# A transformer block on one core: one product for the bias rows of four heads, and two weight blocks split by another engine

## The chip, the cores and the metric

The kernel runs on one core of a Trainium2 chip. The time is that of one execution on the device, in microseconds (us). Three executions took 1603.33, 1603.94 and 1609.25 us; the median is 1603.94.

The core has a matrix engine (TensorE, PE in the profile; its weight loads are PEld), a vector engine (VectorE, DVE), a scalar engine (ScalarE, ACT), a general engine (GpSimd, POOL) and an engine that only issues DMAs (SyncE, SP). Each takes its own instructions in order; between engines semaphores order the work. TensorE's clock is granted at one of two levels, 1.2 and 2.4 GHz; the profile's "PEclk" is the granted share of the higher one.

## The reference, cut to what matters

One decoder layer for 512 tokens of width 1024, all in fp32:

```
a = rmsnorm(x);  dq, dk, dv, rq, rk, rv, rg = split(a @ w_in)
A = differential attention of 4 heads (dq, dk, dv), causal,
    logits + rel_bias[t5_bucket(distance), head]
B = retention of 4 heads (rq, rk, rv), gated by silu(rg)
h = x + concat(A, B) @ w_out
m = rmsnorm(h);  h += peer(m):  scores of m @ Wq against sub-keys, two top-16 lists,
    top-16 of their sums, softmax, sum over experts of gelu(m . u_e) * g_e * v_e
h += sigmoid(rmsnorm(h) @ Wg + bg) * (p @ Wp);  out = rmsnorm(h)
```

The attention's bias depends on the head and on the distance of the two tokens alone. So each head has one row of 640 numbers, a value for each distance, and the 128x512 bias tile of a head is that row, shifted by one place from line to line.

## The kernel before, in words

Every large product is made of three: both operands are split into a high part (a rounded copy, made by ScalarE) and a low part (the rest, a subtraction), and high x high, high x low and low x high are added in PSUM. A weight block (512 KB) is loaded by SP, split, and used by 24 products of 128x512; while one block is multiplied, the next is split (cut_high on ScalarE, cut_low on VectorE) and one further is loaded. The order of each engine's instructions is written out by hand.

After the value projection and the first query projection (project_tile, L214; its products are made at L85), rr holds each token's scale; ScalarE copies it to rT and scales the values (keep_values, L280 to L283). Then come **the bias rows** (L336 to L342). The table relx holds the bias of each bucket and head on 33 partitions, and bucket0 and bucket512 hold for each of 640 distances which bucket it is in (a one for that bucket). relw repeats one head's column of relx 128 times, so that the product of relw[:, h] with the bucket table is the bias row of head h, the same on 128 partitions. For each head there are two products, of 512 and of 128 columns (plain fp32, which TensorE makes in two passes, so two instructions each), into PSUM tiles from a ring of two; ScalarE copies both into bias_s, and POOL's queue writes bias_s to bias_d[h] in DRAM. Later the function table (L375 to L378) loads bias_d[h] back through POOL's queue, with a step of 639 between lines, which makes the shifted 128x512 tile toep; VectorE adds it to the scores (L388).

Then three more projections follow (L344 to L347), each with its scaled copy out of PSUM (keep_dqk, L330 to L333), its split on ScalarE and VectorE, and for queries also two casts on POOL (stack_q, L302). With the second round of steps the attention loop begins: it interleaves the steps of further projections with the scores of one head and 128 queries (scores_of, L380; products at L322).

The query projection of the expert part (**Wq**) has 16 blocks, used from L945 on. Blocks 0 and 1 are loaded and prepared ahead of it, in the output projection, with VectorE. In the loop over blocks, prepare (L735) is called for a block that is two ahead: ScalarE makes the high part (L745), and the low part is made in one of two ways. With `low` = VectorE it is one subtraction (L761). With `low` = GpSimd ScalarE writes the negated block to wl (L758) and POOL issues a DMA that adds the raw block to it (L759):

```
if low is nc.gpsimd:
    nc.scalar.activation(wl, w, AF.Copy, scale=-1.0)
    nc.gpsimd.dma_start(wl.bitcast(F32), w, accum_op=OP.add)
else:
    low.tensor_tensor(wl, w, wh.bitcast(F32), op=OP.subtract)
```

Each turn of the loop then multiplies a block (products, L765), copies its result to qt (ScalarE, L980), multiplies the block before with its sub-keys (score, L948 to L954) and ranks the one before that (rank, top-16 lists on VectorE).

Of the kernel before, what the change touches and what calls it, by code (L numbers as in the profile page):

```python
# [23 lines left out]
F32 = mybir.dt.float32  # L24
# [5 lines left out]
AF = mybir.ActivationFunctionType  # L30
# [5 lines left out]
P = 128  # L36
# [18 lines left out]
def block_kernel(ctx: ExitStack, tc, t):  # L55
    nc = tc.nc

    def pool(name, bufs=1, **kw):
        return tc.tile_pool(name=name, bufs=bufs, reuse_waits="tile", **kw)
# [36 lines left out]
    def operand():  # L96
        return [[ops.tile([P, S], F32R, name=f"x{z}{k}", tag=f"x{z}{k}") for z in "hl"] for k in range(KC)]

    def scaled_split(h, lo, src, gain):

        nc.scalar.activation(h, src, AF.Copy, scale=gain)
        nc.vector.scalar_tensor_tensor(lo, src, gain, h.bitcast(F32), op0=OP.mult, op1=OP.subtract)
# [39 lines left out]
    bias_d = dram.tile([4, P, 640], F32, name="bias_d")  # L142
    blk = [slice(b * P, (b + 1) * P) for b in range(4)]
    halves = [slice(0, S), slice(S, D)]
    with pool("wa", 2, side="right") as wa, pool("sm", 2, side="right") as sm, \
# [67 lines left out]
        with pool("proj", side="right") as pj, pool("att", 2, side="right") as at:  # L213
            def project_tile():  # L214
                ps = mm.tile([P, S], F32, name="ps", tag="mm")
                project(ps, take(), xa, slice(0, S))
                ahead()
                return ps


            relx = pj.tile([33, 4], F32, name="relx")
            nc.gpsimd.memset(relx, -1.0e30)
            nc.gpsimd.dma_start(relx[:32], t["rel_bias"])
            bucket = [(at.tile([33, c1 - c0], F32, name=f"bucket{c0}", tag=tag, **kw), c0, c1)
                      for c0, c1, tag, kw in ((0, 512, "rp", {}), (512, 640, "rx", {"bufs": 3}))]
# [3 lines left out]
            for i, n in enumerate(("lam_q1", "lam_k1", "lam_q2", "lam_k2")):  # L229
                x = t[n]  # L230
# [8 lines left out]
            def fetch_x(i):  # L239
                x = at.tile([P, 2, S], F32, name="pr", tag="pr", bufs=3)  # L240
                if i > 0:
                    nc.sync.dma_start(x, t["xT"][:, 2 * i:2 * i + 2])
                else:
                    raw_w[0] = wa.tile([P, 2, S], F32, name="wraw", tag="wraw")
                    for z in range(2):
                        nc.sync.dma_start(x[:, z], t["xT"][:, z])
                        nc.sync.dma_start(raw_w[0][:, z], blocks[0][0][:, z])
                return x

            steps[:] = 1, 1, 1  # L250
            x = fetch_x(0)
            cut_w[0] = [wa.tile([P, 2, S], F32R, name="w" + z, tag="w" + z, bufs=3) for z in "hl"]
            for i in range(4):
# [8 lines left out]
                x = nx  # L262
# [20 lines left out]
                    nc.scalar.activation(val[which, b], ps[b], AF.Copy, scale=ra[:, b:b + 1])  # L283

            first_q = project_tile()
            relw = at.tile([33, 4, P], F32, name="relw", tag="rp")
            nc.vector.tensor_copy(relw, relx[:, :, None].to_broadcast([33, 4, P]))
            rr = psM.tile([P, S], F32, name="rr", tag="misc")
            token_rows(at.tile([P, 4, P], F32, name="dg", tag="rx", bufs=3), rr, ra)
            rT = pj.tile([P, S], F32, name="rT")  # L290
# [42 lines left out]
                dqk[a, m, z] = yield from (stack_q, stack_k)[z](m, x)  # L333


            for h in range(4):  # L336
                bias_s = at.tile([P, 640], F32, name="bias_s", tag="pr", bufs=3)
                for x, c0, c1 in bucket:
                    pb = psM.tile([P, 512], F32, name="pb", tag="misc")
                    nc.tensor.matmul(pb[:, :c1 - c0], relw[:, h], x, start=True, stop=True)  # L340
                    nc.scalar.activation(bias_s[:, c0:c1], pb[:, :c1 - c0], AF.Copy)
                nc.gpsimd.dma_start(bias_d[h], bias_s)  # L342

            for m, z in ((0, 1), (1, 0), (1, 1)):  # L344
                ps = project_tile()
# [243 lines left out]
            for n in range(17):  # L589
                if n < 16:  # L590
                    h, qb = n // 4, n % 4
# [59 lines left out]
            for n in range(16):  # L651
                h, b = n // 4, n % 4
# [82 lines left out]
        def prepare(u, low):  # L735
            kind, i = u
            w = raw.pop(u)
            if kind == "g":
                for d in range(2):
                    c = slice(d * S, (d + 1) * S)  # L740
                    scaled_split(fin["gh"][i][d], fin["gl"][:, i, c], w[:, c], gains[:, G_PLE, i:i + 1])
                return
            wh = wt.tile([P, D], F32R, name="wh", tag="wh")
            wl = wt.tile([P, D], F32R, name="wl", tag="wl")
            nc.scalar.activation(wh, w, AF.Copy)  # L745
            parts[u] = wh, wl
            if kind == "v":
                gv, av = inputs.pop(u)
                if gv is not None:
                    av3 = av.rearrange("p (z t) -> p z t", t=RUN)  # L750
                    nc.vector.tensor_tensor(av3, gv, av3, op=OP.mult)
                ah = vp[0].tile([P, ND], F32R, name="ah", tag="ah", bufs=2)
                al = vp[0].tile([P, ND], F32R, name="al", tag="al", bufs=2)
                nc.scalar.activation(ah, av, AF.Copy)  # L754
                parts[u] += ah, al
# [6 lines that stand above are left out]
            if kind == "v":  # L762
                nc.vector.tensor_tensor(al, av, ah.bitcast(F32), op=OP.subtract)  # L763
# [157 lines left out]
    with pool("pk") as pk, pool("psG", 2, space=PSUM) as psG, pool("psT", space=PSUM) as psT:  # L921
# [3 lines left out]
        def top16(lists):  # L925
            for v, ix, src, tmp in lists:
                nc.vector.max(v[:, 0:8], src)
            for v, ix, src, tmp in lists:
                nc.vector.match_replace(tmp, v[:, 0:8], src, NEG)
            for v, ix, src, tmp in lists:  # L930
                nc.vector.max(v[:, 8:16], tmp)
            for v, ix, src, tmp in lists:
                nc.vector.max_index(ix[:, 0:8], v[:, 0:8], src)
            for v, ix, src, tmp in lists:
                nc.vector.max_index(ix[:, 8:16], v[:, 8:16], tmp)
# [7 lines left out]
        with pool("qs", 2) as qs:  # L943
            units = [("q", c) for c in range(16)] + [("u", n) for n in range(RAW - 1)]
            loaded, prepared = 2, 2  # L945
            sks, qt, scores = {}, {}, {}

            def score(c):  # L948
                sc = psT.tile([P, 4, P], F32, name="sc", tag="sc")
                for b in range(4):  # L950
                    nc.tensor.matmul(sc[:, b], qt[c][:, b * P:(b + 1) * P], sks[c], start=b == 0, stop=b == 3,  # L951
                                     skip_group_check=True)
                scores[c] = qs.tile([P, 4, P], F32, name="scs", tag="scs", bufs=3)
                nc.scalar.activation(scores[c], sc, AF.Copy)  # L954

            def rank(c):
                ic = qs.tile([P, 4, TOPK], U32, name="ic", tag="ic")
                for b in (0, 2):
                    top16([(vals[:, z, c], ic[:, z], scores[c][:, z],
                            pk.tile([P, P], F32, name="tmp", tag="tmp", bufs=2)) for z in (b, b + 1)])  # L960
                nc.vector.tensor_copy(idx[:, :, c], ic)

            for c in range(16):
                while loaded < min(len(units), c + RAW):
                    load(units[loaded])
                    loaded += 1
                while len(sks) < min(16, c + RAW):
                    k = len(sks)
                    sks[k] = qs.tile([P, P], F32, name="sk", tag="sk", bufs=RAW + 1)
                    nc.sync.dma_start(sks[k], t["sk_t"][k])  # L970
                while prepared < min(len(units), c + 3):
                    prepare(units[prepared], nc.gpsimd if units[prepared][0] == "q" else nc.vector)
                    prepared += 1
                if c == 0:
                    nc.vector.tensor_copy(io2, iof[:, :, None].to_broadcast([P, P, 2]))
                    nc.vector.tensor_copy(pairs.rearrange("p z a k -> p (z a) k"),
                                          prf[:, :3 * TOPK, None].to_broadcast([P, 3 * TOPK, TOPK]))
                products(("q", c))
                qt[c] = qs.tile([P, S], F32, name="q", tag="q")
                nc.scalar.activation(qt[c], made.pop(("q", c)), AF.Copy)  # L980
                if c:
                    score(c - 1)
                if c > 1:
                    rank(c - 2)
            score(15)
            rank(14)
            rank(15)
# [195 lines left out]
        while busy or later or after or n % QUAD:  # L1183
# [23 lines left out]
            while (writes and n >= made_at[writes[0][2]] + 2 and clock["dma"] + LOAD <= clock["pe"] + SLACK):  # L1207
                f, q, g = writes.pop(0)
# [103 lines left out]
    with pool("acc", space=PSUM) as pa:  # L1312
# [43 lines left out]
        loaded, prepared = RAW - 1, 2  # L1356
# [13 lines left out]
        for n, u in enumerate(seq):  # L1370
            while loaded < min(total, n + RAW):
# [4 lines left out]
                if kind == "g" and "gh" not in fin:  # L1376
                    x = operand()
# [10 lines left out]
            if writes and n % W_EVERY == 0:  # L1388
                f, q, g = writes.pop(0)
# [13 lines left out]
            if 0 <= n - end_at < len(ends):  # L1403
                name, b = ends[n - end_at]
# [100 lines left out]
```

## Time and profile before

| | |
|---|---|
| median of three executions | 1603.94 us |
| profiled execution, its own time | 1605.48 us |
| its span, first to last instruction | 1603.7 us |
| mean granted TensorE clock | 0.985 |
| TensorE busy | 1542.4 us, 96% |
| VectorE busy | 1222.3 us, 76% |
| ScalarE busy | 678.9 us, 42% |
| GpSimd busy | 376.2 us, 23% |
| chain that ended last | PE 64%, DMA 13%, issue 11%, DVE 7%, POOL 2%, ACT 2% |

The profile is one execution. A row of the timeline has the start and the duration in us, engine, line of the kernel, operation, what is written and read, shape, and in brackets how long the engine stood before it and for whom. Several like instructions in a row are merged (x4). The ends of matmuls are modelled and overlap, so the distance of two starts is a better measure of a product than its duration.

### The profile page before, as it was taken

To read this page: it belongs to the slowest core of one execution; us is meant where nothing else is said; L and a number is where in the kernel's file an instruction comes from. 1 tells how busy PE (TensorE), PEld (TensorE's weight loads), DVE (VectorE), ACT (ScalarE), POOL (GpSimd) and SP (SyncE) were. 2 spreads that over 40 slices of the span, in tenths; PEclk is the share of its full clock that TensorE was granted. 3 is DMA by queue.
4 is the path that set the end of the run, shared out by engine and by line. 5 is a ranking of instruction groups with operands and counts; after the bars stand their busy time and mean duration, and the time that the engine had idled before them with its cause. 6 is when DMAs were issued, how large, how long until landed. Compare 5 with 4: busy or idle time off the path is not lost.

```text
span 1603.7 us, 22942 instructions
## 1 busy us (share of the span) xinstructions
PE 1542.4 (96%) x8209; PEld 1348.4 (84%) x8209; DVE 1222.3 (76%) x2523; ACT 678.9 (42%) x1077; POOL 376.2 (23%) x311
## 2 busy tenths in 40 slices
PE   8999999899999999999999898989999999999997
PEld 6787877787999999999999776777888888888885
DVE  3576565478998989998866787768888875897655
ACT  5455545444634453454343232323333333354444
POOL 1200000110013203203113444445434320432000
PEclk9899999999999999999999999999999999999998
DMA  6322324774458979987998888889999999899701
GB/s 230 102 76 79 112 99 185 213 176 117 167 187 268 319 219 316 297 283 259 315 295 305 307 301 306 308 288 343 408 386 366 359 328 346 302 401 345 255 28 48
DMA packets 163475, 402.72 MB, mean 251 GB/s; under 512 B 14528, under 2 KB 77259, under 8 KB 163233
## 3 DMA queue, kind: packets, MB, share of 16 engines
q1 hardware_dynamic: 123248, 256.06, 45.3%
q0 software_dynamic: 40112, 145.20, 27.2%
q8 instruction: 64, 1.05, 0.3%
q14 instruction: 51, 0.41, 0.1%
HBM read 350.61 MB, written 42.21 MB: 245 GB/s over the span
## 4 chain that ended last, share of the span: by engine, by line
PE 64%; DMA 13%; issue 11%; DVE 7%; POOL 2%; ACT 2%; SPq 0%; POOLq 0%; DVEq 0%; ACTq 0%
PE ps L85 32%; PE acc L781 19%; DMA row<-in_peer_v_dram,e_sp 7%; DMA row<-in_peer_u_dram,e_sp 4%; PE S L85 3%; POOL row L847 2%; PE S L322 1%; PE ps L517 1%; PE wo L85 1%; DVE wl L761 1%; PE pg L1116 1%; PE pg L1118 1%; DMA wraw<-in_u_t_dram 1%; PE sc L951 1%; DVE yacc L860 1%
## 5 line engine op out<-in xcount | busy, mean ns | idle before, releaser
L85 PE MATMUL ps<-xh,wh 128*128 128x384 f32 (+1 forms) x1312 | 466.4, 355 | 5.3 <-ACT kept L793 3.0
L85 PE MATMUL ps<-xh,wl 128*128 128x384 f32 (+1 forms) x1312 | 459.4, 350 | 7.3 <-DMA wl<-wraw 4.3
L85 PE MATMUL ps<-xl,wh 128*128 128x384 f32 (+1 forms) x1320 | 459.4, 348 | 0.0
L745 ACT ACTIVATE wh<-wraw 128x1024 fp32r<-128x1024 f32 x272 | 286.5, 1054 | 193.2 <-PE ps L85 101.8
L761 DVE TENSOR_TENSOR wl<-wraw,wh 128x1024 fp32r<-128x1024 f32 x258 | 314.6, 1221 | 64.7 <-ACT wh L745 60.0
L85 PEld LDWEIGHTS ps<-xh,wl 128*128 128x128 f32 x1312 | 248.6, 189 | 21.7 <-DMA wl<-wraw 4.8
L85 PEld LDWEIGHTS ps<-xh,wh 128*128 128x128 f32 x1312 | 249.1, 190 | 19.0 <-ACT kept L793 3.3
L847 POOL DMA_INDIRECT row<-in_peer_v_dram,e_sp x128 | 170.8, 1334 | 391.0 <-DVE act L858 309.6
L847 POOL DMA_INDIRECT row<-in_peer_u_dram,e_sp x128 | 169.1, 1321 | 387.4 <-DVE yacc L860 245.9
L85 PEld LDWEIGHTS ps<-xl,wh 128*128 128x128 f32 x1320 | 250.7, 190 | 10.7
L781 PE MATMUL acc<-wl,ah 128*128 128x512 f32 x768 | 240.2, 394 | 14.0 <-DVE wl L761 13.9
L781 PE MATMUL acc<-wh,ah 128*128 128x512 f32 x768 | 240.0, 394 | 9.6 <-ACT ah L754 9.4
L781 PE MATMUL acc<-wh,al 128*128 128x512 f32 x768 | 238.4, 392 | 0.0
L860 DVE SCALAR_TENSOR_TENSOR yacc<-row,act,yacc 128x1024 f32<-128x1024 f32 x128 | 163.9, 1280 | 30.6 <-DMA row<-in_peer_v_dram,e_sp 30.4
L781 PEld LDWEIGHTS acc<-wl,ah 128*128 128x128 f32 x768 | 143.8, 189 | 49.1 <-DVE wl L761 20.0
L858 DVE CUSTOM_DVE_ANT_0 junk<-row,mtok 128x1024 bf16<-128x1024 f32 x128 | 156.1, 1220 | 34.5 <-DMA row<-in_peer_u_dram,e_sp 34.1
L781 PEld LDWEIGHTS acc<-wh,ah 128*128 128x128 f32 x768 | 143.9, 189 | 44.4 <-ACT ah L754 15.6
L781 PEld LDWEIGHTS acc<-wh,al 128*128 128x128 f32 x768 | 143.8, 189 | 32.5 <-DVE al L763 3.2
L754 ACT ACTIVATE ah<-av 128x384 fp32r<-128x384 f32 x104 | 54.6, 525 | 255.0 <-PE acc L781 145.1
L1126 ACT ACTIVATE gs<-pg 128x832 f32<-128x832 f32 x48 | 41.5, 865 | 146.1 <-PE pg L1118 114.2
L763 DVE TENSOR_TENSOR al<-av,ah 128x384 fp32r<-128x384 f32 x104 | 57.7, 554 | 55.5 <-ACT ah L754 55.5
L185 DVE TENSOR_TENSOR wl<-wraw,wh 128x1024 fp32r<-128x1024 f32 x33 | 40.6, 1230 | 29.2 <-ACT wh L179 29.0
(288 smaller groups left out, 1711.6 us busy)
## 6 DMA issues: line engine op xcount, KB each, us to landing
wraw<-in_u_t_dram SPq DMA_DIRECT2D x128, 512.0 KB
wraw<-in_peer_v_dram SPq DMA_DIRECT2D x128, 512.0 KB
gv<-g_d SPq DMA_DIRECT2D x26, 768.0 KB
g_d<-gs SPq DMA_DIRECT2D x24, 576.0 KB
a<-av SPq DMA_DIRECT2D x72, 192.0 KB
av<-a SPq DMA_DIRECT2D x72, 192.0 KB
wraw<-in_w_in_t_dram SPq DMA_DIRECT2D x16, 512.0 KB
wraw<-in_wq_t_dram SPq DMA_DIRECT2D x16, 512.0 KB
```

What stands on the lines that cost most here:

```text
L85: nc.tensor.matmul(out, a, b, start=first and k == 0, stop=last and k == n - 1)
L185: nc.vector.tensor_tensor(cut_w[k][1], raw_w.pop(k), cut_w[k][0].bitcast(F32), op=OP.subtract)
L322: nc.tensor.matmul(out, *((a, b) if q_first else (b, a)), start=n == 0, stop=n == 1)
L745: nc.scalar.activation(wh, w, AF.Copy)
L754: nc.scalar.activation(ah, av, AF.Copy)
L761: low.tensor_tensor(wl, w, wh.bitcast(F32), op=OP.subtract)
L763: nc.vector.tensor_tensor(al, av, ah.bitcast(F32), op=OP.subtract)
L781: nc.tensor.matmul(acc[b][d], a[:, c], bb[:, d * S:(d + 1) * S], start=f, stop=l)
L847: nc.gpsimd.indirect_dma_start(out=rows[n], out_offset=None, in_=t[table], in_offset=bass.IndirectOffsetOnAxis(ap=e_sp[:, r:r + 1], axis=0))
L858: nc.vector.tensor_tensor_reduce(junk, row, mtok, 1.0, 0.0, OP.mult, OP.add, act[:, r:r + 1])
L860: nc.vector.scalar_tensor_tensor(yacc, row, act[:, r:r + 1], yacc, op0=OP.mult, op1=OP.add)
L1126: nc.scalar.activation(gs[0][:, :, t0:t0 + 8], pgi[:, KEEP:], AF.Copy, scale=2.0 ** -15)
```

## The change

The bias rows: relw repeats each head's column 32 times instead of 128, so that the four heads together fill 128 columns. One product with each bucket table then gives the rows of all heads, head h on partitions 32h to 32h + 31. Two products and two copies serve four heads. Each head's 32 equal lines are written four times, to make the 128 lines of bias_d[h]: 16 DMAs of 32 lines.

Wq: the way over GpSimd is taken only from `prepared` = 4 on. Blocks 0 and 1 are prepared elsewhere, so blocks 2 and 3 change their way.

```diff
-            relw = at.tile([33, 4, P], F32, name="relw", tag="rp")
-            nc.vector.tensor_copy(relw, relx[:, :, None].to_broadcast([33, 4, P]))
+            relw = at.tile([33, 4, 32], F32, name="relw", tag="rp")
+            nc.vector.tensor_copy(relw, relx[:, :, None].to_broadcast([33, 4, 32]))
...
+            bias_s = at.tile([P, 640], F32, name="bias_s", tag="pr", bufs=3)
+            for x, c0, c1 in bucket:
+                pb = psM.tile([P, 512], F32, name="pb", tag="misc")
+                nc.tensor.matmul(pb[:, :c1 - c0], relw.rearrange("p h r -> p (h r)"), x, start=True, stop=True)
+                nc.scalar.activation(bias_s[:, c0:c1], pb[:, :c1 - c0], AF.Copy)
             for h in range(4):
-                bias_s = at.tile([P, 640], F32, name="bias_s", tag="pr", bufs=3)
-                for x, c0, c1 in bucket:
-                    pb = psM.tile([P, 512], F32, name="pb", tag="misc")
-                    nc.tensor.matmul(pb[:, :c1 - c0], relw[:, h], x, start=True, stop=True)
-                    nc.scalar.activation(bias_s[:, c0:c1], pb[:, :c1 - c0], AF.Copy)
-                nc.gpsimd.dma_start(bias_d[h], bias_s)
+                for q in range(4):
+                    nc.gpsimd.dma_start(bias_d[h, 32 * q:32 * q + 32], bias_s[32 * h:32 * h + 32])
...
-                    prepare(units[prepared], nc.gpsimd if units[prepared][0] == "q" else nc.vector)
+                    prepare(units[prepared], nc.gpsimd if units[prepared][0] == "q" and prepared > 3 else nc.vector)
```

## Rows read from the trace of the kernel before

**Rows 1.** Busy time by stretch; columns named in the first line.
```profile
core 0: us, PE busy (x) PEld busy (x) DVE busy (x) ACT busy (x) POOL busy (x), PEclk, DMA share, GB/s
37.95:49.27 11.32, 8.59 (x17) 3.98 (x17) 0.00 (x0) 5.41 (x12) 1.63 (x3) 0.66 0.22 87
...
73.97:277.30 203.33, 201.34 (x1057) 162.04 (x1056) 132.76 (x319) 108.22 (x259) 9.80 (x16) 1.00 0.34 113
288.48:303.11 14.63, 9.68 (x34) 7.61 (x35) 4.97 (x33) 5.32 (x8) 2.66 (x3) 0.77 0.85 202
...
303.10:309.50 6.40, 6.40 (x35) 5.43 (x34) 4.80 (x33) 3.09 (x4) 0.86 (x1) 1.00 0.49 134
```

**Rows 2.** Timeline of TensorE: bias products and the first scores.
```profile
37.87 1.34 PE L340 MATMUL pb<-bucket,relw 33*128 33x512 f32 x4
41.42 2.40 PE L340 MATMUL pb<-bucket,relw 33*128 33x512 f32 x4 [2.21 <-ACT bias_s L341]
...
73.97 0.22 PE L322 MATMUL S<-k,q 128*128 128x128 f32 x1
```

**Rows 3.** Chain that ended last, in order of time: start, us, what.
```profile
49.34 24.79 PE ps L85 x96
```

**Rows 4.** Timeline of ScalarE: the first head's bias copies, the first q.
```profile
40.75 0.79 ACT L341 ACTIVATE bias_s<-pb 128x512 f32<-128x512 f32 x2
...
52.55 1.28 ACT L301 ACTIVATE q<-dx 64x512 fp32r<-64x512 f32 x2 [1.89 <-DVE dx L332]
```

**Rows 5.** Timeline of VectorE.
```profile
50.69 1.22 DVE L185 TENSOR_TENSOR wl<-wraw,wh 128x1024 fp32r<-128x1024 f32 x1 [14.52 <-ACT wh L179]
51.83 0.68 DVE L332 SCALAR_TENSOR_TENSOR dx<-ps,rT 128x512 f32<-128x512 f32 x1
...
74.99 0.29 DVE L388 CUSTOM_DVE_ANT_0 pr<-S,toep 128x128 f32<-128x128 f32 x1
```

**Rows 6.** Timeline of POOL.
```profile
2.02 1.08 POOL L227 DMA_DIRECT2D bucket<-in_bucket_dram  x2
...
41.83 0.55 POOL L342 DMA_DIRECT2D bias_d<-bias_s  x1 [36.03 <-ACT bias_s L341]
...
53.24 2.15 POOL L302 CAST q<-q 64x512 fp32r<-64x512 f32 x2 [2.70 <-ACT q L301]
...
66.80 0.54 POOL L378 DMA_DIRECT2D toep<-bias_d  x1
```

**Rows 7.** Stretches of one us, last with traffic of a bias write and table load.
```profile
43.40:44.40 1.00, 0.74 (x3) 0.45 (x3) 0.00 (x0) 0.77 (x2) 0.00 (x0) 0.50 0.33 128
...
68.80:69.80 1.00, 1.00 (x6) 0.84 (x5) 0.61 (x1) 0.35 (x1) 0.00 (x0) 1.00 0.29 115
```

**Rows 8.** The same view, ahead of the second head's products.
```profile
39.30:41.40 2.10, 0.00 (x0) 0.00 (x0) 0.00 (x0) 2.10 (x5) 0.00 (x0) 1.00 0.00 0
```

**Rows 9.** Chain that ended last, at blocks 2 and 3 of Wq.
```profile
288.87 6.14 DMA wl<-wraw
...
295.05 8.06 PE ps L85 x22
303.11 0.89 PE sc L951 x8
304.00 5.47 PE ps L85 x24
```

**Rows 10.** Timeline of TensorE at block 2 of Wq.
```profile
289.10 1.16 PE L951 MATMUL sc<-sk,q 128*128 128x128 f32 x8 [0.63 <-ACT q L980]
...
295.05 0.79 PE L85 MATMUL ps<-xh,wl 128*128 128x512 f32 x1 [4.33 <-DMA wl<-wraw]
```

**Rows 11.** Timeline of ScalarE at block 2 of Wq.
```profile
286.56 1.06 ACT L745 ACTIVATE wh<-wraw 128x1024 fp32r<-128x1024 f32 x1 [7.36 <-DMA wraw<-in_wq_t_dram]
...
288.47 0.58 ACT L980 ACTIVATE q<-ps 128x512 f32<-128x512 f32 x1
```

**Rows 12.** Timeline of POOL at block 2 of Wq.
```profile
288.87 0.92 POOL L759 DMA_DIRECT2D wl<-wraw  x1 [61.37 <-ACT wl L758]
```

**Rows 13.** Waits of TensorE from 450 to 1600 us: total, times, longest.
```profile
PE acc L781 <- DVE wl L761: 13.9, 7, 4.9
```

## The prediction, made before the change was timed

> **What bounds the kernel now.** I read the stretch table first, then the chain of waits and the engines' timelines around the two edited places, then the waits. TensorE is all but full from 73.97 to 277.30 us (201.34 of 203.33 us, granted clock 1.00), but not in the two stretches that the diff touches: from 37.95 to 49.27 us it is busy 8.59 of 11.32 us at a clock of 0.66, from 288.48 to 303.11 us 9.68 of 14.63 us at 0.77 [rows 1]. In the first, one head's bias products take 1.34 us warm; then TensorE stands 2.21 us for ScalarE's copy of the bias row, and each further head runs at the lower clock (2.40 us) [rows 2]. The projections behind them have no other reason to be late: the chain goes straight from the last bias product into 96 products, 24.79 us [rows 3]. In the second, TensorE stands 0.63 us for ScalarE's copy of q and 4.33 us for an accumulating DMA [rows 10], 6.14 us from issue to landing on the chain, and the 22 products after it take 8.06 us where 24 take 5.47 us warm [rows 9]. Both are stalls of the engine that bounds the neighbouring stretches, so what they give up should reach the end.
>
> **The bias rows.** Removed: three of four heads, so 6 of 8 bias products (12 of 16 TensorE instructions, the fp32 product being two passes) and 6 of 8 ScalarE copies. Kept: one product pair, same shapes (33 partitions in, 128 out). TensorE should be through with it when head 0 is now, at 37.87 + 1.34 = 39.21 us, the half that waits for rT included [rows 2]. Next in TensorE's order come four blocks of 24 products (three projections and the first block's worth of steps that the attention loop interleaves) and then the first scores. Warm, a block is 5.47 us [rows 9], so the scores start at 39.21 + 21.88 = 61.09 us instead of 73.97 [rows 2]: **12.9 us**. Of these 2.9 are the cold products (24.79 against 21.88) and 10.1 the wait and three heads; lower end for the clock, if it falls all the same: 10.0.
>
> Can the others keep up? ScalarE is done with both bias copies at 40.75 + 0.79 = 41.54 us [rows 4]. Behind them wait the high part of the next weight block (1.06, a row of the same form in [rows 11]), then VectorE's low part (1.22) and the scaled copy that frees the first projection's PSUM buffer (0.68) [rows 5]: ready at about 44.5 us, wanted at 39.21 + 5.47 = 44.68. That is tight; a slip costs its own length, which I bound at 0 to 1 us. The later blocks have 1 to 3 us by the same count. The raw weights that these need are in SBUF by then: from 39.30 to 41.40 us nothing is moved [rows 8].
>
> Added: POOL issues 16 DMAs (32 partitions, 80 KB) instead of 4. A 33-partition DMA costs 1.08/2 = 0.54 us of POOL, a 128-partition one 0.55 [rows 6], so 16 take 8.6 us, from 41.83 to about 50.5, all of one bias tile instead of four spread over 8 us. Behind them in POOL's order stand the casts of two q tiles (2.15 us a pair, [rows 6]) and then the load of the first Toeplitz table. ScalarE gives the first q at about 45.8 us (44.5 and 1.28, [rows 4]) and, two blocks on by the same count, the second at about 54, so the first casts are held some 5 us by the issues and the second ones not at all: done near 56, the table issued then, its traffic over 3.0 us after the start of the issue (66.80 to 69.80, [rows 6, 7]), so there by about 59. The scores want the casts at 61.1, VectorE's bias addition wants the table about 1 us later (74.99 against 73.97 now, [rows 2, 5]). So the queue is hidden, with some 3 us to spare. Bounds of an issue: below 0.5, above 0.92, POOL's dearest here [rows 12]; at 0.92 the issues end at 56.5, the casts at 60.8, and the table is in at 63.8, 1.7 us after it is wanted, so 1.7 us at the most. I take 0, since the nearest rows are plain DMAs of 33 and 128 partitions.
>
> The bias tile's buffer is taken again at the third score tile, some 10 us after the scores start; the 16 writes are over long before. VectorE's fill of relw gets shorter (128 elements for 512), beside TensorE's first projection: nothing.
>
> **The first blocks of Wq.** Blocks 0 and 1 already go to VectorE, so the condition changes blocks 2 and 3. Removed: two ScalarE copies (of the size of the 1.06 us one in [rows 11]), two POOL issues, two accumulating DMAs. Added: two VectorE subtractions of 1.22 us. Block 2: its high part still waits for the raw weights, 286.56 + 1.06 = 287.62 us [rows 11]; VectorE, idle there, has the low part by 288.9. The copy of q is then next on ScalarE, done by 288.2 instead of 289.05. TensorE ends block 1 at 288.47, so the score product (0.89) starts at once, block 2 follows at 289.4 and ends at 294.85 instead of 303.11 [rows 9, 10]: **8.25 us** (0.63 and 4.33 of waiting, 3.0 of cold products, and small change). Block 3's low part, behind ScalarE's q copy and 1.06, is ready by 290.5 and wanted at 296. VectorE also has the top-16 lists then, 4.80 us of work in a period of 6.40 us [rows 1], so it is not late.
>
> What is late next? Block 4 keeps its accumulating DMA. ScalarE can hand it over at about 292.3, POOL takes 0.92 [rows 12], and with 6.14 us [rows 9] it lands near 299; TensorE wants it near 302.4. So 3.4 us of cover; if the landing took over 10 us, the stall would come back there.
>
> **Sum.** 12.9 + 8.25 = 21.1 us. The profiled execution took 1605.48 us (span 1603.70), so 1584.3; the median of the runs is 1.5 us below that execution, hence 1582.8 us; **1583 us**. Behind the edits TensorE is the full engine up to 277 us [rows 1], and from 450 us its largest sum of waits is 13.9 us, for VectorE's low parts [rows 13]. VectorE takes its start from TensorE's results and from loads that begin when a buffer comes free, so both start earlier by the same amount, and I let the whole gain through.
>
> **The rivals.**
>
> The writes go one at a time (the other side). If each bias write had to land before the next one starts, POOL would stand in them. A write of 320 KB now takes 41.83 to 44.40, 2.57 us [rows 6, 7]; 16 of these end at 83.0, two pairs of casts bring 87.3, the table 90.3, and VectorE's first addition is 15.3 us later than 74.99. Less 8.25, that is 7 us slower: 1611 for the median. It decides from 2.1 us a write, (74.99 + 8.25 - 3.0 - 4.3 - 41.83)/16; at 6.14, as for the accumulating DMA, the kernel would be over 60 us slower. Against it: two DMAs of POOL in 1.08 us [rows 6]. For it: no row shows so many at once from one tile. 5%. The Trainium skill, "DMA: Bandwidth & Descriptors", section "Anatomy of one DMA — SWDGE (gpsimd) path", gives each DMA from POOL a fixed cost of about 2.0 us whatever its size, which speaks against cutting four writes into sixteen. By its fit the write of 320 KB is 2.75 us (an estimate), near the trace's 2.57 to the last traffic; 16 of 80 KB in turn would be 35 us, and the kernel within 1 us of now. The page lays that cost on the completion, which writes in flight together share; so it bears on this rival only if they do go one at a time.
>
> The stall moves to block 4: the accumulating DMA lands late among the loads, and 4.33 + 3.05 us of the second part come back: 1590. For it: DMA engines are nearly full from 288.48 us (share 0.85, [rows 1]); against it, two of these DMAs less. 8%.
>
> The clock falls all the same in the first stretch, as TensorE runs thin products for 2.3 us before the projections: 2.9 us come back, 1586. Against it: the clock is still 1.00 there now and falls only after 2.21 us of standing still. 5%.
>
> The first part is lost later, in a wait that doesn't move with TensorE: only 8.25 us remain, 1595.7. Against it: 201.34 of 203.33 us of TensorE's time between the two edits are busy [rows 1]. 4%.
>
> More than counted, because waits of the later stretches shrink too: below 1576. 3%.
>
> **How the numbers follow.** My forecast 75%, the rivals as above. The range 1576 to 1592 holds the forecast with 1.7 us for POOL, 1 us for the tight handover and 3 us of scatter, and the cases at 1586 and 1590; left out are 12%. 0.5%, 8 us, is about what can be told from no change. Faster takes the forecast, 1586, 1590, the case below 1576 and half of the one at 1595.7: 0.93. Same takes the other half and the cheaper end of the serial writes: 0.04. Slower is the rest of these: 0.03.
>
> **What would show it.** Right: two bias copies on ScalarE, TensorE's next projection beginning near 39.2 us at a clock of 1.00, the first scores near 61; 16 POOL issues of about 0.55 us; TensorE without a wait for the low part of blocks 2 and 4, and block 2 ending some 21 us earlier than 303.11. Wrong: VectorE's first bias addition waiting for the table or TensorE's scores for POOL's casts; a wait for an accumulating DMA at block 4; or a distance from block 2's end to the end of the span that is more than some 3 us longer than now.

## The result, and the profile after

The changed kernel took 1586.6 us (median of six runs, 1581.09 to 1590.82) against 1604.12 us (median of six runs of the kernel before); the ratio is 0.9885, 95% interval 0.9861 to 0.9909. Two further measurements, each beside the kernel before on its own chip, gave 0.9881 (0.9859 to 0.9903) and 0.9875 (0.9856 to 0.9894). So it is faster by 1.2%, 18 to 20 us; 21.1 us were forecast, a ratio of 0.9868, inside all three intervals.

Busy time by stretch (columns as in [rows 1]): the bias products, the four blocks behind them, the way to Wq, and the 14.6 us from the end of block 1 of Wq, the length that block 2 took before; now block 3 fits into it as well:

```profile
38.69:40.04 1.35, 1.35 (x6) 0.74 (x5) 0.00 (x0) 1.24 (x3) 0.00 (x0) 1.00 0.15 58
40.04:61.89 21.85, 21.85 (x97) 18.05 (x97) 14.08 (x24) 13.61 (x20) 12.72 (x21) 1.00 0.50 146
61.89:265.16 203.27, 201.32 (x1057) 162.05 (x1055) 132.76 (x319) 108.22 (x258) 9.82 (x16) 1.00 0.35 113
276.38:290.99 14.61, 14.61 (x78) 12.48 (x77) 12.19 (x72) 8.06 (x12) 1.80 (x2) 1.00 0.78 208
```

TensorE is full at a clock of 1.00 in both edited stretches, where [rows 1] has 0.66 and 0.77; the stretch between them is as long as it was (203.27 against 203.33 us).

Its timeline at the first place, and the chain of waits over both:

```profile
38.69 1.34 PE L339 MATMUL pb<-bucket,relw 33*128 33x512 f32 x4
...
61.89 0.22 PE L322 MATMUL S<-k,q 128*128 128x128 f32 x1
```

```profile
38.76 1.27 PE pb L339 x4
40.04 22.01 PE ps L85 x96
...
276.38 0.89 PE sc L952 x8
277.27 5.46 PE ps L85 x24
282.74 0.89 PE sc L952 x8
```

From the first bias product to the first scores it is 61.89 - 38.69 = 23.20 us, before 73.97 - 37.87 = 36.10 [rows 2]: 12.9 us less. From the end of block 1 to the end of block 2 it is 282.74 - 276.38 = 6.36 us, before 303.11 - 288.47 = 14.64 [rows 9, 11]: 8.3 us less. The first bias product itself comes 0.8 us later than before. It arises ahead of the edited places: TensorE's waits for its first operands, in the first 40 us, add up to 6.6 us in this profile and to 5.9 before.

The other engines at the first place, ScalarE, VectorE and POOL:

```profile
41.57 0.79 ACT L340 ACTIVATE bias_s<-pb 128x512 f32<-128x512 f32 x2
42.20 1.11 ACT L179 ACTIVATE wh<-wraw 128x1024 fp32r<-128x1024 f32 x1
```

```profile
44.48 0.68 DVE L332 SCALAR_TENSOR_TENSOR dx<-ps,rT 128x512 f32<-128x512 f32 x1
...
62.91 0.29 DVE L389 CUSTOM_DVE_ANT_0 pr<-S,toep 128x128 f32<-128x128 f32 x1
```

```profile
42.65 5.98 POOL L343 DMA_DIRECT2D bias_d<-bias_s  x12 [36.83 <-ACT bias_s L340]
49.92 1.96 POOL L343 DMA_DIRECT2D bias_d<-bias_s  x4 [1.30 <-DMA bias_d<-bias_s]
51.92 2.31 POOL L302 CAST q<-q 64x512 fp32r<-64x512 f32 x2
54.42 2.15 POOL L302 CAST q<-q 64x512 fp32r<-64x512 f32 x2 [0.18 <-ACT q L301]
56.52 0.55 POOL L379 DMA_DIRECT2D toep<-bias_d  x1
```

Sixteen issues take 0.50 us each, but after the twelfth POOL stands 1.30 us for an earlier write. The five other profiles with 16 writes have the same stand ahead of the thirteenth, 1.00 to 1.30 us. The casts end at 56.57 us, 5.3 us before the scores, and VectorE's first addition starts at 62.91 without a wait.

### The profile page after: what moved, and what is told of

It reads as the page before. It is cut to its first block, busy times and chain, and to the rows that moved or that the text cites. A ratio compares the mean times of both kernels' runs of the same rounds, so it can differ in the third digit from the quotient of the medians.

```text
span 1584.7 us, 22924 instructions
## 1 busy us (share of the span) xinstructions
PE 1530.4 (97%) x8197; PEld 1342.8 (85%) x8197; DVE 1223.3 (77%) x2525; ACT 674.6 (43%) x1069; POOL 376.4 (24%) x321
## 4 chain that ended last, share of the span: by engine, by line
PE 56%; issue 16%; DMA 14%; DVE 8%; POOL 3%; ACT 1%; SPq 0%; POOLq 0%; DVEq 0%; ACTq 0%
PE ps L85 26%; PE acc L782 18%; DMA row<-in_peer_v_dram,e_sp 6%; DMA row<-in_peer_u_dram,e_sp 6%; POOL row L848 3%; PE S L85 3%; DVE wl L762 2%; DMA wraw<-in_u_t_dram 2%; PE S L322 1%; PE ps L518 1%; PE wo L85 1%; DVE junk L859 1%; PE sc L952 1%; DVE yacc L861 1%; PE pg L1117 1%
## 5 line engine op out<-in xcount | busy, mean ns | idle before, releaser
L762 DVE TENSOR_TENSOR wl<-wraw,wh 128x1024 fp32r<-128x1024 f32 x260 | 317.0, 1220 | 71.4 <-ACT wh L746 69.8
L782 PE MATMUL acc<-wl,ah 128*128 128x512 f32 x768 | 239.9, 394 | 9.8 <-DVE wl L762 9.7
L782 PE MATMUL acc<-wh,ah 128*128 128x512 f32 x768 | 239.7, 394 | 8.6 <-ACT ah L755 8.4
L782 PE MATMUL acc<-wh,al 128*128 128x512 f32 x768 | 238.4, 392 | 0.0
L782 PEld LDWEIGHTS acc<-wl,ah 128*128 128x128 f32 x768 | 143.7, 189 | 45.4 <-DVE wl L762 15.9
L782 PEld LDWEIGHTS acc<-wh,ah 128*128 128x128 f32 x768 | 144.2, 189 | 42.3 <-ACT ah L755 13.2
L782 PEld LDWEIGHTS acc<-wh,al 128*128 128x128 f32 x768 | 143.6, 189 | 32.3 <-DVE al L764 3.1
L752 DVE TENSOR_TENSOR av<-gv,av 128x384 f32<-128x384 f32 x104 | 57.3, 551 | 3.6 <-DMA av<-a 3.6
```

The lines of the kernel that those rows point to most:

```text
L782: nc.tensor.matmul(acc[b][d], a[:, c], bb[:, d * S:(d + 1) * S], start=f, stop=l)
```

## The experiments

"Before" and "changed" name the two kernels; ratios are to before, with 95% intervals. Distances within a profile are counted from the first bias product to the first scores (36.1 us before, 23.2 changed), since the start of the kernel scatters.

**One part alone.** The changed kernel with the old condition at Wq:

```diff
-prepare(units[prepared], nc.gpsimd if units[prepared][0] == "q" and prepared > 3 else nc.vector)
+prepare(units[prepared], nc.gpsimd if units[prepared][0] == "q" else nc.vector)
```

> Only the bias rows are changed; all Wq blocks from 2 on keep their accumulating DMA. Theory (two separate stalls of TensorE, each passed through to the end): first scores 12.9 us earlier counted from the first bias product, 1604.1 - 12.9 = 1591 us; TensorE still waits some 4.3 us for the accumulating DMA at block 2. Rival (a later stretch takes back what the first part gives): the first scores come as early, but the distance from there to the end is 3 us or more longer than before, 1594 to 1604 us.

Measured: 1594.16 us, ratio 0.9928 (0.9905 to 0.9952), 11.6 us by the ratio; the theory had 1591, and the rival begins at 1594. TensorE waits 3.7 us for the accumulating DMA at block 2. In this profile the distance is 24.7 us, not 23.2: the load of x for the norm came late, TensorE stood 1.6 us ahead of rr, and the clock fell behind it. The chain of waits, the waits of TensorE, and two stretches of this kernel:

```profile
25.93 7.22 DMA xt<-in_x_dram
...
40.92 23.55 PE ps L85 x96
```

```profile
PE rr L132 <- DVE dg L131: 1.6, 1, 1.6
...
PE ps L85 <- DMA wl<-wraw: 3.7, 1, 3.7
```

```profile
39.60:41.00 1.40, 1.40 (x6) 0.79 (x5) 0.00 (x0) 1.31 (x3) 0.00 (x0) 0.93 0.81 316
41.00:46.50 5.50, 5.50 (x18) 4.41 (x19) 1.83 (x2) 3.61 (x7) 2.96 (x6) 0.71 0.24 53
```

The rival's sign is there, too: from the first scores to the end of the span it is 1534.4 us (1598.7 - 64.31), 4.7 us longer than before (1603.7 - 73.97 = 1529.7). But the profiled execution was the slowest of the six (1600.48 us), and the excess lies in the late part, on which more below. This run alone doesn't settle the rival.

**The other part alone**, the condition in the kernel before (the diff above, read the other way, applied to it).

> Only blocks 2 and 3 of Wq are changed; the bias rows are made head by head as before. Theory: block 2 ends 8.3 us earlier counted from the end of block 1, 1604.1 - 8.3 = 1596 us. Rival (the stall moves on to block 4, whose DMA is now the first of its kind): TensorE waits 1 to 5 us at block 4, 1599 to 1602 us. Rival (later stretches take it back): no wait at block 4, yet 1600 us or more.

Measured: 1596.73 us, ratio 0.9943 (0.9924 to 0.9961), 9.1 us, as the theory had it. TensorE has no wait at blocks 2 or 4, and block 2 takes 5.50 us:

```profile
290.90 5.50 PE ps L85 x24
```

The two parts are 11.6 and 9.1 us, together 20.7, near the forecast of 21.1, though each interval is some 3 to 4 us wide to either side.

**The changed kernel again**, beside these two, unedited.

> The changed kernel once more, beside its two halves on one chip. Theory: the halves add up, 12.9 + 8.3 = 21.2 us less than before, so 1583 to 1585 us, and 0.9868 as a ratio. Rival (about 2 us are given back in the late part, as the first profile of it shows between the first and the last expert product): 1586 to 1588 us again, with that stretch longer by 2 us again.

Measured: 1585.76 us, ratio 0.9881, between the theory's time and the rival's. The stretch from the first to the last expert product (L781, L782) was 680.2 us in the profile of before and 682.1 in the first one of the changed kernel; here it is 678.4:

```profile
863.90:1544.10 680.20, 653.62 (x2984) 548.73 (x2984) 532.20 (x692) 243.29 (x338) 245.34 (x185) 0.99 0.89 324
843.20:1525.30 682.10, 655.27 (x2986) 550.28 (x2985) 531.83 (x692) 243.05 (x339) 243.05 (x185) 0.99 0.89 323
841.90:1520.30 678.40, 651.91 (x2984) 547.60 (x2983) 531.60 (x693) 243.32 (x339) 241.93 (x185) 0.99 0.89 325
```

In a third profile of the changed kernel, the last run below, it is 685.4 us. So one and the same kernel has 678.4 to 685.4 us here; the thirteen profiles of this study lie between 678.0 and 687.6, among them 685.5 with the first part alone and 685.8 with the second. The 2 us "given back" in the first profile, and the 5 us of the run with the first part alone, are within that scatter, and the rival isn't borne out. What makes the stretch scatter was not tried.

**What the first part gained.** The kernel before with the bias copies made by VectorE, which is idle there:

```diff
-nc.scalar.activation(bias_s[:, c0:c1], pb[:, :c1 - c0], AF.Copy)
+nc.vector.tensor_copy(bias_s[:, c0:c1], pb[:, :c1 - c0])
```

> The kernel before, all four heads made one by one, but their eight copies out of PSUM made by VectorE, which is idle there, instead of ScalarE, which is busy with the values. Theory (the wait for ScalarE and the lower clock that follows it are two thirds of the first part's gain, the three heads' products themselves one third, 3 x 1.34 = 4.0 us): TensorE doesn't stand more than about 0.7 us at a time, keeps the higher clock, and the first scores come 7 to 9 us earlier: 1595 to 1597 us. Rival (the products are the cost, not the wait): 0 to 3 us earlier, 1601 to 1604 us.

Measured: 1603.18 us, ratio 0.9984 (0.9968 to 1.0000). The theory fell, and the time is the rival's: the distance is 33.3 us, only 2.8 less. TensorE's timeline and one stretch:

```profile
38.82 1.34 PE L340 MATMUL pb<-bucket,relw 33*128 33x512 f32 x4
40.73 1.34 PE L340 MATMUL pb<-bucket,relw 33*128 33x512 f32 x4 [0.56 <-DVE bias_s L341]
42.63 2.27 PE L340 MATMUL pb<-bucket,relw 33*128 33x512 f32 x4 [0.56 <-DVE bias_s L341]
45.26 2.50 PE L340 MATMUL pb<-bucket,relw 33*128 33x512 f32 x4 [0.35 <-DVE bias_s L341]
```

```profile
42.60:45.20 2.60, 2.27 (x4) 0.96 (x4) 0.86 (x3) 0.18 (x1) 0.54 (x1) 0.56 0.50 197
```

A wait stays, since each head needs both PSUM buffers of the ring and its first product waits for the copy of the head before; and the clock falls all the same, though no stand is longer than 0.56 us. So is it the waits, or the products? The next kernel has the same 16 product instructions, arranged so that no product stands for a copy:

```diff
+pc = psM.tile([P, 4, P], F32, name="pc", tag="misc")
+for h in range(4):
+    nc.tensor.matmul(pc[:, h], relw[:, h], bucket[1][0], start=h == 0, stop=h == 3, skip_group_check=True)
+bias_t = at.tile([P, 4, P], F32, name="bias_t", tag="pr", bufs=3)
+nc.vector.tensor_copy(bias_t, pc)
+nc.gpsimd.dma_start(bias_d[:, :, 512:640].rearrange("h p c -> p h c"), bias_t)
 for h in range(4):
...
+    nc.tensor.matmul(pb, relw[:, h], bucket[0][0], start=True, stop=True)
+    nc.vector.tensor_copy(bias_s, pb)
+    nc.gpsimd.dma_start(bias_d[h, :, 0:512], bias_s)
```

> The kernel before, four heads made one by one, but TensorE has no copy to wait for: the four 128-column products share one PSUM tile, so that each 512-column product has a buffer of its own while the one before is copied, and VectorE copies. The products themselves are the same 16 instructions. Theory A (what the first part gained was the waits between heads, and the clock that falls with them; thin products in an unbroken row keep it): products over in about 4 x 1.34 = 5.4 us at a clock of 1.00, first scores 36.1 - 4.0 - 23.2 = 8.9 us earlier counted from the first bias product, some 1596 us. Theory B (the products themselves let the clock fall, as they did with stands of only 0.56 us when VectorE copied): clock 0.5 from the second or third head on, 3 to 5 us earlier, some 1600 us.

Measured: 1600.07 us, ratio 0.9949 (0.9930 to 0.9967). Its chain and stretches:

```profile
39.26 1.08 PE pc L338 x8
40.35 4.80 PE pb L345 x8
45.15 24.04 PE ps L85 x96
```

```profile
38.50:41.00 2.50, 2.50 (x17) 1.76 (x16) 0.75 (x2) 1.70 (x4) 0.00 (x0) 1.00 0.66 210
41.00:44.00 3.00, 3.00 (x6) 1.13 (x6) 1.46 (x3) 2.16 (x4) 1.88 (x3) 0.78 0.39 122
44.00:47.00 3.00, 3.00 (x7) 1.54 (x6) 2.50 (x4) 0.00 (x0) 1.08 (x2) 0.50 0.59 225
```

TensorE's record has no gap from 38.5 to 47 us, and still the granted clock goes from 1.00 to 0.78 to 0.50, the lower of its two levels: theory B. (The weight loads of these products do wait for VectorE's copies, 2.1 us in all, but as long as the clock is 1.00 the large products begin 0.43 to 0.54 us after one another, so next to nothing of that reaches them.) The distance is 69.05 - 39.26 = 29.8 us, 6.3 less than before, somewhat more than the 3 to 5 us of theory B. The other 6.6 us up to the changed kernel are the products of three heads, the last of them at the lower clock (1.08 + 4.80 - 1.27 = 4.6) and the projections behind them at the fallen clock (24.04 - 22.01 = 2.0).

**How much POOL's queue can take.** The changed kernel with twice the writes:

```diff
-for q in range(4):
-    nc.gpsimd.dma_start(bias_d[h, 32 * q:32 * q + 32], bias_s[32 * h:32 * h + 32])
+for q in range(8):
+    nc.gpsimd.dma_start(bias_d[h, 16 * q:16 * q + 16], bias_s[32 * h:32 * h + 16])
```

> The changed kernel with 32 writes of 16 lines instead of 16 of 32. Theory (POOL's queue has some 3 us of cover behind 16 writes, at 0.5 us an issue): POOL ends the issues 8 us or more later, near 60 us, the casts end near 64.5, the scores wait for them and VectorE's first addition for the table, 5 to 8 us later than in the changed kernel: 1591 to 1595 us. Rival (the queue doesn't matter, the table's wait is taken up behind it): 1585 to 1588 us.

Measured: 1595.0 us, ratio 0.9906 (0.9877 to 0.9935). POOL, VectorE and TensorE:

```profile
41.94 5.80 POOL L343 DMA_DIRECT2D bias_d<-bias_s  x12 [36.11 <-ACT bias_s L340]
...
58.04 3.65 POOL L302 CAST q<-q 64x512 fp32r<-64x512 f32 x4
61.63 0.56 POOL L379 DMA_DIRECT2D toep<-bias_d  x1
```

```profile
64.71 0.29 DVE L389 CUSTOM_DVE_ANT_0 pr<-S,toep 128x128 f32<-128x128 f32 x1 [1.35 <-DMA toep<-bias_d]
```

```profile
68.50 0.33 PE L410 MATMUL pt<-ident,pr 128*128 128x128 f32 x1 [1.46 <-DVE pr L402]
```

Counted from the first bias product the last issue ends 6.8 us later than in the changed kernel (57.99 - 37.98 against 51.88 - 38.69) and the table is issued 5.8 us later. The table is now what VectorE waits for, and TensorE waits for VectorE: the third scores come 35.7 us after the first bias product (37.98 to 73.69), 31.7 in the changed kernel (38.69 to 70.42). So 4 us, a little under the 5 to 8 that I expected, since the issues were over at 58 us and not at 60, and four casts took 3.65 us in a row. I had expected the first scores to be late, too; they weren't, the table was. By the ratio, too, this kernel is 4 us slower than the changed one (0.9906 against 0.9881); the median's further 4 us aren't told apart from scatter by four runs and this interval.

The other way, one write for each head, which reads its 32 lines four times:

```diff
+nc.gpsimd.dma_start(bias_d[h].rearrange("(q p) c -> p q c", p=32),
+                    bias_s[32 * h:32 * h + 32, None, :].to_broadcast([32, 4, 640]))
```

> The changed kernel with one write for each head instead of four: the DMA reads the head's 32 lines four times. POOL has 4 issues of about 0.55 us again, behind one pair of products. Theory (16 issues are hidden behind ScalarE's and VectorE's work): POOL free of them 6 us earlier, the first casts 5 us earlier, the first scores where they are (23.2 us after the first bias product), same time as the changed kernel, 1584 to 1588 us. Rival (the issues or the 80 KB writes do cost something): 2 us or more faster.

Measured: 1584.46 us, ratio 0.9864 (0.9844 to 0.9885), beside 0.9875 (0.9856 to 0.9894) for the changed kernel on the same chip: no difference that can be told. The four issues take 2.23 us, and the distance stays at 23.2 us. Sixteen writes are hidden; there is nothing in them to gain that the runs could tell.

**Which blocks of Wq matter.** Two kernels differ from the changed one in the number in `prepared > 3`: 2 (block 2 alone goes to VectorE), and 15 (all blocks do).

> The changed kernel with block 2 alone split by VectorE, blocks 3 and on by accumulating DMA. Theory (block 2's stall was the whole of the second part; block 3's DMA is wanted some 6 us after its issue and lands about then): 0 to 2 us slower than the changed kernel, TensorE waits under 1.5 us at block 3: 1586 to 1588 us. Rival (the stall only moves by a block): TensorE waits 3 to 5 us at block 3 and its clock falls, 1591 to 1594 us.

Measured: 1586.07 us, ratio 0.9874 (0.9846 to 0.9901). TensorE's wait there:

```profile
PE ps L85 <- DMA wl<-wraw: 1.1, 1, 1.1
```

Block 2 was nearly all of the second part; block 3 is worth 1.1 us, below what the runs tell apart.

> The changed kernel with every block of Wq split by VectorE, no accumulating DMA. Theory (behind block 2 TensorE is the bound, and VectorE has 4.80 + 1.22 = 6.02 us of work in 6.36): same time as the changed kernel, 1585 to 1588 us, 0.988 of before. Rival (VectorE, in order, ranks late and starts its own chain behind the query projection later): slower than the changed kernel by 3 to 15 us. Rival (ScalarE and DMA freed): 2 us or more faster.

Measured: 1585.47 us, ratio 0.9866 (0.9843 to 0.9889): no difference to the changed kernel that can be told. VectorE is busy 6.14 of 6.40 us in a period; it keeps up, but with nothing to spare:

```profile
291.00:297.40 6.40, 6.40 (x34) 5.44 (x33) 6.14 (x37) 2.18 (x4) 0.00 (x0) 1.00 0.27 92
```

**A late load covered.** On top of one write for each head, the second projection goes ahead of rr and the bias products:

```diff
 first_q = project_tile()
+second = project_tile()
...
-    ps = project_tile()
+    ps = second if (m, z) == (0, 1) else project_tile()
```

> As the kernel with one write for each head, but the second projection is put ahead of the token scales (rr) and the bias products, so that a late load of x for the norm is covered by 5.5 us of projection. In the profiles so far TensorE stood 0 to 1.6 us for rr, and with 1.6 us the clock fell behind it (0.71 over the next 5.5 us). Theory: no stand at rr and no fall of the clock in any profile, and 1 us on average gained, at most 3: 1583 to 1586 us. Rival (rT comes too late for the third projection, whose PSUM buffer the scaled copy of the first one frees): TensorE waits 1 us or more there, 1586 to 1590 us.

Measured: 1585.45 us, ratio 0.9873 (0.9854 to 0.9891). No stand at rr, clock 1.00; but TensorE waits 0.7 us for the scaled copy instead, the rival's wait, though shorter than its 1 us:

```profile
PE ps L85 <- DVE dx L333: 0.7, 1, 0.7
```

Nothing is gained that can be told.

**The changed kernel a third time**, beside these two, unedited.

> The changed kernel a third time, on the chip of the two others. Theory (scatter of the late part and of the loads at the start, nothing systematic): 1583 to 1588 us, ratio 0.986 to 0.990.

Measured: 1586.92 us, ratio 0.9875, as expected.

No kernel of the study beats the changed one by more than the intervals.

## Why the prediction was right, step by step

- *Bias rows, 12.9 us*: 36.10 to 23.20 us, 12.9. The row of one head's products and the warm block of 24 carried it. The four blocks took 22.01 us for 21.88.
- *ScalarE and VectorE just keep up*: the first projection's buffer was free at 44.48 + 0.68 = 45.16 us, wanted at 40.04 + 5.47 = 45.51. No stand, with 0.35 us to spare.
- *16 issues of 0.54 us, hidden, casts done near 56, some 3 us to spare*: 0.50 us each, casts done at 56.57. I had left out that POOL would stand 1.30 us for an earlier write, a small piece of the rival that the writes go one at a time. It did no harm, since the second pair of casts waited for ScalarE's q all the same (0.18 us). In the kernel before, traffic of the table ended 3.0 us after its issue [rows 6, 7], so with 56.52 it was there near 59.5, 3.4 us before VectorE; with 32 writes, where the table is 5.8 us later, VectorE did wait. Apart from that stand, no issue in this profile waited for an earlier write: sixteen went out in 9.2 us. The Trainium skill, "DMA: Bandwidth & Descriptors", section "Anatomy of one DMA — SWDGE (gpsimd) path", lays most of the fixed cost of a DMA, about 2.0 us, on its completion. The rows agree: sixteen of them in turn would be 32 us (an estimate from the page's figure).
- *Wq, 8.25 us*: 8.3, and no stall at block 4, whose issue was at 280.16 us, 9.8 us before its block began at 290.00.
- *Behind the edits everything starts earlier by the same amount*: from the first bias product to the first expert product it was 826.0 us before (37.87 to 863.9) and 804.5 after (38.69 to 843.2), 21.5 us less. From the end of block 2 to the end of the span it is 1302.0 us, 1.4 longer than before (1300.6) and under the 3 us that I had named as a sign of being wrong. What the medians lack of 21.1 us, 1 to 3 us, is within the intervals.
- *The clock*: here a reason of mine was wrong, with the number right. I wrote that it falls only after 2.21 us of standing still. It fell in a row of bias products without a stand, too. In the changed kernel the products are over in 1.3 us, a dense projection follows, and the clock stayed at 1.00, but not always: with a stand of 1.6 us ahead of rr it fell to 0.71 over the next 5.5 us, which cost 1.5 us of the distance (24.7 against 23.2). My rival for this had 2.9 us and 5%, and no stand in it. Its price was twice what the one fall cost; its chance was perhaps too low, as 1 profile of the changed bias rows in 8 (without the one where rr was moved) shows such a fall. That the profiles of the changed kernel itself kept the clock is in part luck: TensorE stood only 0 to 0.64 us ahead of rr in them.

## What to carry to other kernels

A short stage of thin products (here 33 partitions in) can cost TensorE more than its own time: here 3 heads of 1.3 us each were worth 12.9 us, with the waits for PSUM copies and the clock that stayed low for 6 us behind them. Filling the partitions of the output with several small products at once took nearly all of it away here. When one DMA is on the path at the start of a stage, an idle engine that does the same work there (one subtraction of 1.2 us) is worth the whole stall, here 8.3 us; further on, where the same DMA has a period of 6.4 us as cover, the change was worth nothing that the runs could tell.

## What was not expected of the hardware

The granted clock fell from 1.00 to 0.50 while the record of TensorE's row of fp32 products on 33 partitions had no gap (38.5 to 45.2 us). Whether that is due to the few partitions or to the plain fp32 form, which the projections around them don't have, was not tried. POOL's DMA issue costs 0.50 us for 80 KB and 0.49 for 40 KB, and stood for an earlier write after twelve of 80 KB in all six profiles (1.00 to 1.30 us); with 40 KB writes its stands were 0.2 to 0.3 us. What sets that stand was not tried. The load of x for the norm lands between about 30 and 33 us from run to run; TensorE's stand ahead of rr is 0 to 1.6 us with it, and the first bias product begins between 37.9 and 39.6 us (without the kernel where rr was moved).
